# A four-layer diffusion trunk in fp32: norming shared by two engines, epilogue banks released sooner, adaLN chunks placed anew

## The chip, the cores and the metric

The kernel runs on one core of a Trainium2 chip. The metric is the device time of one execution in microseconds (us); the figure for the kernel before is the median of three runs. The engines are TensorE (PE), VectorE (DVE), ScalarE (ACT), GpSimd (POOL) and SyncE (SP), which here only issues loads and stores.

## What is computed

One inference step of a trunk with 128 context tokens and 256 latent tokens (384 columns), D = 1024, four layers. The token mixers are a chunked gMLP (layers 0 and 3), a pooling mixer (layer 1) and a windowed attention (layer 2); each is followed by a gated ConvFFN. Cut to what matters here:

```python
def ada_params(cond, w, b):
    m = jax.nn.silu(cond) @ w + b
    return jnp.split(m[:, None, :], 6, axis=-1)

def conv_ffn(h, w_in, conv_w, conv_b, w_out):
    a, u = jnp.split(h @ w_in, 2, axis=-1)
    ap = jnp.pad(a, ((0, 0), (1, 1), (0, 0)))
    a = ap[:, :-2] * conv_w[0] + ap[:, 1:-1] * conv_w[1] + ap[:, 2:] * conv_w[2] + conv_b
    return (jax.nn.gelu(a) * u) @ w_out
...
        sh1, sc1, gt1, sh2, sc2, gt2 = ada_params(cond, w_ada[i], b_ada[i])
        h = rms_norm(x, g_mix[i]) * (1 + sc1) + sh1
...
        x = x + gt1 * y
        h = rms_norm(x, g_ffn[i]) * (1 + sc2) + sh2
        x = x + gt2 * conv_ffn(h, w_ffn_in[i], ffn_conv_w[i], ffn_conv_b[i], w_ffn_out[i])
```

Context and latent tokens have their own `cond`, so every adaLN vector has two columns.

## The kernel before, in words

Activations lie transposed: x is eight blocks k of 128 features by 384 tokens. All weights are cut by the host into 582 chunks of 128x1024 fp32 (512 KB) in one list, `chunk_plan`, and SP loads them in that order into five raw buffers (`load`, a buffer is free again when its reader is done). To keep fp32 accuracy, a chunk is split: ScalarE copies it to fp32r (`whi`, line 347), VectorE subtracts (`wlo`, line 354), four buffers each; activations are split the same way, and `mm3` (line 669) makes three products, whi x hi, wlo x hi, whi x lo. `w_get` hands out a split chunk and keeps the splits three chunks ahead.

adaLN weights are chunks of the same list that need no split. An "ad" chunk is read by VectorE, two multiplications with a sum per chunk (`ada_dve`, line 389). An "ap" chunk is multiplied on TensorE, four products of 32 columns (`ada_pe`, line 407), its row being turned at the end; its raw buffer is held until TensorE's program comes to it. The table `ADA` says which chunks (kind, layer, which of the six vectors, which of eight blocks) go into which phase; `weave` spreads them between the phase's weight chunks, and `EDGES` says how many weight chunks at its begin and end stay free of them. Phases are named (layer, name): gv, gu and go are the gMLP's, fi is the ffn's first product, fo its second.

The ffn (`ffn`) makes 22 blocks f of a and u, 128 features each; a pair of PSUM banks (pa, pu) holds one f, and there are six such banks. A step of an f is 48 products. To start before the norm of x is known, f = 0, 1 (four "fr" chunks, two blocks k in each) and f = 2 run on raw h, which is x times the gain, with two more columns in which the shift is carried; rows of these three are scaled by rbs, the reciprocal root mean square, in the epilogue. At k = stat_k the sum of squares is taken over the partitions by products with ones (`stats`, line 530: last square and accumulator apart, six matmuls, two passes each) and turned into a diagonal R; at stat_k + 2 `spread` (line 545) gives rbs to all partitions. From then on `norm` writes normed h, block by block (`put_act`: VectorE x times rbs, line 578; ScalarE gain and shift, line 580, and the fp32r part, line 581; VectorE the rest, line 582), for f = 3 to 21. Blocks are done in pairs: two puts, then two rests.

The epilogue of an f stands in the instruction order of the next f: `epi_a` (f < 3: lines 695 and 699 scale a and u out of the banks, line 697 copies the two shift columns of a), `epi_b` (the convolution, lines 710 to 716, named ct), `epi_c` (gelu; gg, line 726, reads u in its bank; for f < 3 line 730 reads the two shift columns of u in its bank), then gg is split. Since f = 0 and 1 come out together, the epilogues run two f behind until f = 8, where one step holds two of them. So f+3 takes the banks of f.

At the start SP loads x, three weights and the parameters; cond goes through Silu, squares of x are summed, and the first block's shift and gain come from `a0` products on TensorE.

Of the kernel before, what the change touches and what calls it, by code (L numbers as in the profile page):

```python
# [1655 lines left out]
```

## Time and profile before

| | us |
|---|---|
| median of 3 runs | 1843.94 (1841.29 to 1845.10) |
| the profiled execution, its own time | 1845.28 |
| its span, first to last instruction | 1843.5 |
| TensorE busy in it | 1762.9 (96%) |
| VectorE busy | 1383.0 (75%) |
| ScalarE busy | 884.9 (48%) |
| mean granted clock of TensorE | 0.983 of 2.4 GHz |

The profile is one execution. Busy time is the share in which an engine has an instruction under way; a wait is idle time, put down to the instruction that ended it. Times inside the profile count from the span's start. fp32 products appear as two passes each, products of fp32r as one.

### The profile page before, as it was taken

To read this page: it belongs to the slowest core of one execution; us is meant where nothing else is said; L and a number is where in the kernel's file an instruction comes from. 1 tells how busy PE (TensorE), PEld (TensorE's weight loads), DVE (VectorE), ACT (ScalarE), POOL (GpSimd) and SP (SyncE) were. 2 spreads that over 40 slices of the span, in tenths; PEclk is the share of its full clock that TensorE was granted. 3 is DMA by queue.
4 is the path that set the end of the run, shared out by engine and by line. 5 is a ranking of instruction groups with operands and counts; after the bars stand their busy time and mean duration, and the time that the engine had idled before them with its cause. 6 is when DMAs were issued, how large, how long until landed. Compare 5 with 4: busy or idle time off the path is not lost.

```text
span 1843.5 us, 26653 instructions
## 1 busy us (share of the span) xinstructions
PE 1762.9 (96%) x10128; PEld 1683.5 (91%) x10128; DVE 1383.0 (75%) x2364; ACT 884.9 (48%) x1637; POOL 1.8 (0%) x30
## 2 busy tenths in 40 slices
PE   7999989999999699999998989999999999899999
PEld 5799989999998699899777979999988999899999
DVE  5887969888985688888688678877776776676632
ACT  3644354444444644542468564543354444654531
POOL 0000000000000000000000000000000000000000
PEclk9999999999999899999999999999999999899999
DMA  8864635565662255566550335555546344244441
GB/s 323 279 210 150 206 113 184 187 202 189 234 218 97 92 194 196 192 202 226 198 177 13 126 106 192 193 167 200 183 147 208 115 138 149 103 154 162 136 137 63
DMA packets 87635, 311.62 MB, mean 169 GB/s; under 512 B 10450, under 2 KB 10962, under 8 KB 87252
## 3 DMA queue, kind: packets, MB, share of 16 engines
q1 hardware_dynamic: 87364, 309.92, 49.7%
q8 instruction: 79, 1.29, 0.3%
q14 instruction: 48, 0.39, 0.1%
q10 hardware_dynamic: 144, 0.01, 0.0%
HBM read 308.06 MB, written 1.84 MB: 168 GB/s over the span
## 4 chain that ended last, share of the span: by engine, by line
PE 68%; DVE 19%; ACT 9%; issue 3%; DMA 1%; DVEq 0%; ACTq 0%
PE mm L669 51%; DVE junk L389 6%; PE mm L834 6%; DVE wlo L354 5%; DVE ct L716 3%; ACT whi L347 2%; ACT nt L580 2%; PE S L669 1%; PE mm L878 1%; ACT hb L581 1%; ACT gg L725 1%; DVE gl L587 1%; PE adaT L669 1%; PE S L1109 1%; DMA wraw<-wts 1%
## 5 line engine op out<-in xcount | busy, mean ns | idle before, releaser
L669 PE MATMUL mm<-hb,whi 128*128 128x384 f32 (+1 forms) x4064 | 902.3, 341 | 49.7 <-DVE gg L730 27.0
L669 PEld LDWEIGHTS mm<-hb,whi 128*128 128x128 f32 x4064 | 731.9, 191 | 57.2 <-issue 28.4
L354 DVE TENSOR_TENSOR wlo<-wraw,whi 128x1024 fp32r<-128x1024 f32 (+2 forms) x390 | 466.7, 1201 | 223.8 <-ACT whi L347 222.7
L347 ACT ACTIVATE whi<-wraw 128x1024 fp32r<-128x1024 f32 (+2 forms) x390 | 400.1, 1034 | 276.4 <-PE mm L669 185.2
L669 PE MATMUL mm<-hb,wlo 128*128 128x384 f32 (+1 forms) x2032 | 527.1, 340 | 4.4 <-DVE wlo L354 4.3
L389 DVE SCALAR_TENSOR_TENSOR junk<-wraw,condb 128x1024 bf16<-128x1024 f32 x320 | 391.0, 1222 | 8.4 <-ACT condb L1574 2.7
L669 PEld LDWEIGHTS mm<-hb,wlo 128*128 128x128 f32 x2032 | 373.4, 191 | 6.9 <-DVE wlo L354 6.9
L725 ACT ACTIVATE gg<-ct 128x128 f32<-128x128 f32 (+1 forms) x152 | 47.0, 356 | 273.4 <-DVE ct L716 273.4
L669 PE MATMUL mm<-gh,whi 128*128 128x384 f32 x448 | 124.1, 338 | 2.5 <-ACT whi L347 2.5
L669 PE MATMUL mm<-gh,wlo 128*128 128x384 f32 x448 | 124.0, 338 | 0.8 <-DVE wlo L354 0.8
L669 PE MATMUL mm<-gl,whi 128*128 128x384 f32 x448 | 123.8, 337 | 0.0
L716 DVE SCALAR_TENSOR_TENSOR ct<-ab,par,ct 128x385 f32<-128x385 f32 x176 | 108.8, 620 | 7.9 <-ACT ct L714 4.2
L605 ACT ACTIVATE hb<-x,A 128x128 fp32r<-128x128 f32 x96 | 43.2, 457 | 102.9 <-DVE x L462 92.0
L834 PE MATMUL mm<-whi,hb 128*128 128x512 f32 x320 | 87.5, 399 | 0.0
L669 PEld LDWEIGHTS mm<-gh,whi 128*128 128x128 f32 x448 | 82.2, 189 | 2.9 <-ACT whi L347 2.9
L669 PEld LDWEIGHTS mm<-gh,wlo 128*128 128x128 f32 x448 | 82.4, 189 | 1.1 <-DVE wlo L354 1.1
L669 PEld LDWEIGHTS mm<-gl,whi 128*128 128x128 f32 x448 | 82.3, 189 | 0.0
L726 DVE TENSOR_TENSOR gg<-mm,gg 128x384 f32<-128x384 f32 x76 | 42.4, 558 | 47.4 <-ACT gg L725 46.7
L834 PEld LDWEIGHTS mm<-whi,hb 128*128 128x128 f32 x320 | 60.6, 190 | 15.9 <-ACT rb L1560 0.8
L714 ACT ACTIVATE ct<-ab,par 128x385 f32<-128x385 f32 x88 | 62.7, 712 | 3.4
L462 DVE SCALAR_TENSOR_TENSOR x<-mm,prm,x 128x128 f32<-128x128 f32 x92 | 33.6, 411 | 27.4 <-PE mm L669 27.3
L607 DVE SCALAR_TENSOR_TENSOR hb<-x,A,hb 128x128 fp32r<-128x128 f32 x96 | 40.2, 418 | 9.9 <-ACT hb L605 0.9
(276 smaller groups left out, 1648.5 us busy)
## 6 DMA issues: line engine op xcount, KB each, us to landing
wraw<-wts SPq DMA_DIRECT2D x562, 512.0 KB, 3.9
wraw<-wts SPq DMA_DIRECT2D x12, 256.0 KB, 3.1
wraw<-wts SPq DMA_DIRECT2D x8, 384.0 KB, 4.2
x<-x SPq DMA_DIRECT2D x4, 384.0 KB, 4.5
mx<-mix SPq DMA_DIRECT2D x1, 1280.0 KB, 8.1
y<-x SPq DMA_DIRECT2D x3, 384.0 KB, 4.2
condb<-condb SPq DMA_DIRECT2D x1, 1024.0 KB, 8.3
ws<-a_w_s SPq DMA_DIRECT2D x2, 512.0 KB, 4.0
```

The source lines that it names most:

```text
L347: nc.scalar.activation(hi[:, :n], t[:, :n], AF.Copy)
L354: nc.vector.tensor_tensor(out=lo[:, :n], in0=t[:, :n], in1=hi[:, :n].bitcast(F32), op=ALU.subtract)
L389: nc.vector.scalar_tensor_tensor(out=self.junk.bitcast(BF16), in0=w, scalar=1.0, in1=self.condb[:, c, :], op0=ALU.mult, op1=ALU.mult, accu ...
L580: nc.scalar.activation(t[:, t0:t1], t[:, t0:t1], AF.Identity, scale=A[:, k, c:c + 1], bias=sh[:, k, c:c + 1])
L605: nc.scalar.activation(self.hh[:, d, t0:t1], self.x[:, d, t0:t1], AF.Copy, scale=A[:, d, c:c + 1])
L607: nc.vector.scalar_tensor_tensor(out=self.hl[:, d, t0:t1], in0=self.x[:, d, t0:t1], scalar=A[:, d, c:c + 1], in1=self.hh[:, d, t0:t1].bitc ...
L669: nc.tensor.matmul(o, w[:, c:c + nw], r, start=(first and p == 0), stop=(last and p == 2))
L714: nc.scalar.activation(t, ab[:, 1:T + 2], AF.Identity, scale=cw[1], bias=cb)
L716: nc.vector.scalar_tensor_tensor(out=t, in0=ab[:, i:i + T + 1], scalar=cw[i], in1=t, op0=ALU.mult, op1=ALU.add)
L725: nc.scalar.activation(g[:, t0:t1], t[:, t0 + c:t1 + c], GELU)
L726: nc.vector.tensor_tensor(out=g, in0=u, in1=g, op=ALU.mult)
L834: nc.tensor.matmul(ps[n][i], hs, w[p == 1][:, c:c + 512], start=(k == 0 and p == 0), stop=(k == 7 and p == 2))
```

## The change

1. `norming` writes normed h. Even blocks k are made as before; for odd ones VectorE multiplies by gain and rbs (two pieces, since context and latent differ), ScalarE adds the shift into the fp32r part, and VectorE makes the rest in two pieces. The rest of block k-1 is issued behind the put of block k.
2. `stat_k` goes from 3 to 2, and in layer 1 from 6 to 4.
3. The last square is added to acc on VectorE (`add_square`), so `stats` takes three matmuls for six, in the four ffns and layer 3's gMLP.
4. be is four wide: ScalarE copies the shift columns of u as well, and line 730's successor reads them from there.
5. The step with two epilogues is f = 5 and no longer f = 8.
6. `ADA` and `EDGES`: (0,go) 9 to 12 ad and 8 ap, (0,fi) 26 to 18, (0,fo) 19 to 16, (1,fi) 24 to 18, (1,fo) 16 to 22 ad; 582 chunks as before.
7. At the start: ones first, Silu's table loaded by a dummy, the small constant sel loaded from ScalarE's queue, and 25, 3 and 5 fp32 products of ones into a spare bank ahead of the first a0 products, the stats and the first turned row.

```diff
 ADA = {
@@
-    (0, "go"): [("ad", 0, 3, 2, 8), ("ad", 0, 5, 0, 3)],
-    (0, "fi"): [("ad", 0, 5, 3, 8), ("ad", 1, 1), ("ad", 1, 2), ("ad", 1, 0, 0, 5)],
-    (0, "fo"): [("ad", 1, 0, 5, 8), ("ad", 1, 4), ("ad", 1, 3)],
-    (1, "fi"): [("ad", 1, 5), ("ad", 2, 1), ("ad", 2, 0)],
-    (1, "fo"): [("ad", 2, 4), ("ad", 2, 3)],
+    (0, "go"): [("ad", 0, 3, 2, 8), ("ad", 0, 5, 0, 6), ("ap", 1, 1)],
+    (0, "fi"): [("ad", 0, 5, 6, 8), ("ad", 1, 2), ("ad", 1, 0)],
+    (0, "fo"): [("ad", 1, 4), ("ad", 1, 3)],
+    (1, "fi"): [("ad", 1, 5), ("ad", 2, 1), ("ad", 2, 0, 0, 2)],
+    (1, "fo"): [("ad", 2, 0, 2, 8), ("ad", 2, 4), ("ad", 2, 3)],
@@
-EDGES = {(0, "gv"): (2, 1), (0, "go"): (5, 0), (3, "gv"): (5, 2), "fi": (8, 4), (3, "go"): (5, 2)}
+EDGES = {(0, "gv"): (2, 1), (0, "go"): (5, 0), (3, "gv"): (5, 2), "fi": (8, 2), (3, "go"): (5, 2)}
+WARM = (25, 3, 5)
@@
+    def add_square(self, pr):
+        self.nc.vector.tensor_tensor(out=pr["acc"], in0=pr["acc"], in1=pr["sq"], op=ALU.add)
@@
-    def put_act(self, k, A, rbs, hi, lo, sh):
+    def put_one(self, k, A, rbs, hi, lo, sh, act):
         nc = self.nc
         t = self.tmp.tile([128, T], F32, tag="sq", name="nt")
...
         for c, (t0, t1) in enumerate(GRPS):
+            nc.vector.scalar_tensor_tensor(out=t[:, t0:t1], in0=self.x[:, k, t0:t1], scalar=A[:, k, c:c + 1],
+                                           in1=rbs[:, t0:t1], op0=ALU.mult, op1=ALU.mult)
+            nc.scalar.activation(hi[:, k, t0:t1], t[:, t0:t1], AF.Identity, bias=sh[:, k, c:c + 1])
+        def last():
+            for c, (t0, t1) in enumerate(GRPS):
+                nc.vector.scalar_tensor_tensor(out=lo[:, k, t0:t1], in0=t[:, t0:t1], scalar=sh[:, k, c:c + 1],
+                                               in1=hi[:, k, t0:t1].bitcast(F32), op0=ALU.add, op1=ALU.subtract)
+        return last
@@
-                be = self.tmp.tile([128, 2], F32, tag="be", name="be")
-                nc.scalar.activation(be, pa[:, T:TE], AF.Copy)
+                be = self.tmp.tile([128, 4], F32, tag="be", name="be")
+                nc.scalar.activation(be[:, 0:2], pa[:, T:TE], AF.Copy)
+                nc.scalar.activation(be[:, 2:4], pu[:, T:TE], AF.Copy)
@@
-                return f, a1, be, u1, pu[:, T:TE]
+                return f, a1, be, u1, be[:, 2:4]
@@
-            def norm(n):
-                ks, to_norm[:] = to_norm[:n], to_norm[n:]
-                for i in range(0, len(ks), 2):
-                    for lo in [self.put_act(k, pr["A"], rbs, nh, nl, sh) for k in ks[i:i + 2]]:
-                        lo()
+            def norming():
+                last = None
+                for k in range(KD):
+                    this = self.put_one(k, pr["A"], rbs, nh, nl, sh, k % 2 == 0)
+                    if last is not None:
+                        last()
+                    last = this
+                    yield
+                last()
+            steps = norming()
+            def norm(n):
+                for _ in range(n):
+                    next(steps, None)
+            self.add_square(pr)
@@
-                        R = self.diag(self.stats(pr["acc"], pr["sq"]))
+                        R = self.diag(self.stats(pr["acc"]))
@@
-                now, prev = (prev, []) if f == 8 else (prev[:1], prev[1:])
+                now, prev = (prev, []) if f == 5 else (prev[:1], prev[1:])
@@
         nc.scalar.dma_start(cin, a["cond"])
+        nc.scalar.dma_start(self.cst[:, 512:514], a["cst"][:, 512:514])
...
-        nc.sync.dma_start(self.cst[:, 512:514], a["cst"][:, 512:514])
         self.load()
+        nc.vector.memset(self.ones, 1.0)
...
+        nc.scalar.activation(self.tmp.tile([128, 1], F32, tag="dmy", name="dmy", bufs=1), self.ones[:, 0:1], AF.Silu)
+        spare = self.bank("spare")
+        def warm(n):
+            for _ in range(WARM[n]):
+                nc.tensor.matmul(spare[:, 0:128], self.ones, self.ones, start=True, stop=True)
+        warm(0)
...
+        def first_stats():
+            warm(1)
+            r.append(self.stats(acc))
+        a0_mm(0, first_stats)
+        warm(2)
@@
-            pr = self.ffn(l, pr, follow, 6 if kind == 1 else 3)
+            pr = self.ffn(l, pr, follow, 4 if kind == 1 else 2)
```

The order of VectorE at the norming of layer 2's ffn, before (nt and hb are the put and the rest, a and u the first epilogue):

```order
L578 TENSOR_TENSOR nt<-x,rbs 128x384 x2
L582 TENSOR_TENSOR hb_84<-nt,hb_84 128x384 x2
L354 TENSOR_TENSOR wlo<-wraw,whi 128x1024
L578 TENSOR_TENSOR nt<-x,rbs 128x384 x2
L582 TENSOR_TENSOR hb_84<-nt,hb_84 128x384 x2
L578 TENSOR_TENSOR nt<-x,rbs 128x384 x2
L582 TENSOR_TENSOR hb_84<-nt,hb_84 128x384 x2
L578 TENSOR_TENSOR nt<-x,rbs 128x384 x2
L582 TENSOR_TENSOR hb_84<-nt,hb_84 128x384 x2
L695 TENSOR_TENSOR a_2457<-mm,rbs 128x384
L699 TENSOR_TENSOR u_2461<-mm,rbs 128x384
L354 TENSOR_TENSOR wlo<-wraw,whi 128x1024
```

And after the change, the same place:

```order
L585 TENSOR_TENSOR nt<-x,rbs 128x384
L598 SCALAR_TENSOR_TENSOR hb_84<-nt,prm,hb_84 128x128
L598 SCALAR_TENSOR_TENSOR hb_84<-nt,prm,hb_84 128x256
L592 SCALAR_TENSOR_TENSOR nt<-x,A,rbs 128x128
L592 SCALAR_TENSOR_TENSOR nt<-x,A,rbs 128x256
L589 TENSOR_TENSOR hb_84<-nt,hb_84 128x384
L585 TENSOR_TENSOR nt<-x,rbs 128x384
L598 SCALAR_TENSOR_TENSOR hb_84<-nt,prm,hb_84 128x128
L598 SCALAR_TENSOR_TENSOR hb_84<-nt,prm,hb_84 128x256
L592 SCALAR_TENSOR_TENSOR nt<-x,A,rbs 128x128
L592 SCALAR_TENSOR_TENSOR nt<-x,A,rbs 128x256
L589 TENSOR_TENSOR hb_84<-nt,hb_84 128x384
```

The puts of two blocks stood together, then their rests; now each rest stands behind the next block's put, and every second block has two instructions for one.

The order of VectorE from the third epilogue's end into the step that holds two, layer 2, after the change (line 736 is ct, 746 gg, 391 an adaLN chunk, 606 the rest of gg):

```order
L356 TENSOR_TENSOR wlo<-wraw,whi 128x1024
L606 TENSOR_TENSOR gl<-gg,gh 128x384
L356 TENSOR_TENSOR wlo<-wraw,whi 128x1024
L391 SCALAR_TENSOR_TENSOR junk,prm<-wraw,condb 128x1024 x2
L736 SCALAR_TENSOR_TENSOR ct<-ab_2354,par,ct 128x385 x2
L736 SCALAR_TENSOR_TENSOR ct<-ab_2353,par,ct 128x385 x2
L746 TENSOR_TENSOR gg<-mm,gg 128x384 x2
L356 TENSOR_TENSOR wlo<-wraw,whi 128x1024
L606 TENSOR_TENSOR gl<-gg,gh 128x384 x2
L356 TENSOR_TENSOR wlo<-wraw,whi 128x1024
```

Before, f=5's step held one ct and one gg, and the like rows with two of them stood at f=8:

```order
L354 TENSOR_TENSOR wlo<-wraw,whi 128x1024
L389 SCALAR_TENSOR_TENSOR junk,prm<-wraw,condb 128x1024 x2
L716 SCALAR_TENSOR_TENSOR ct<-ab_2250,par,ct 128x385 x2
L716 SCALAR_TENSOR_TENSOR ct<-ab_2251,par,ct 128x385 x2
L726 TENSOR_TENSOR gg<-mm,gg 128x384 x2
L354 TENSOR_TENSOR wlo<-wraw,whi 128x1024
L389 SCALAR_TENSOR_TENSOR junk,prm<-wraw,condb 128x1024 x2
L587 TENSOR_TENSOR gl<-gg,gh 128x384 x2
```

The two epilogues at once now belong to f = 3 and 4 and no longer to f = 6 and 7.

The order of TensorE at the kernel's begin, after the change (spare is the bank of the products of ones, psa the a0 products, cs the stats, a0T the turned row):

```order
L1534 MATMUL spare<-ones 128x128 x25
L1550 MATMUL psa<-wraw,cond 32x256 x4
L1534 MATMUL spare<-ones 128x128 x3
L536 MATMUL cs<-ones,acc 128x1 x3
L1550 MATMUL psa<-wraw,cond 32x256 x4
L1534 MATMUL spare<-ones 128x128 x5
L1564 MATMUL a0T<-cst,a0row 128x2 x2
L551 MATMUL mm<-R,ones 128x384
L1550 MATMUL psa<-wraw,cond 32x256 x8
```

Line 1534's rows are new there; the others kept their order.

## Rows read from the trace of the kernel before

**Rows 1.** The page: busy times, VectorE's group of line 389, the weights' DMA issues.

```profile
PE 1762.9 (96%) x10128; PEld 1683.5 (91%) x10128; DVE 1383.0 (75%) x2364; ACT 884.9 (48%) x1637; POOL 1.8 (0%) x30
...
L389 DVE SCALAR_TENSOR_TENSOR junk<-wraw,condb 128x1024 bf16<-128x1024 f32 x320 | 391.0, 1222 | 8.4 <-ACT condb L1574 2.7
...
wraw<-wts SPq DMA_DIRECT2D x562, 512.0 KB, 3.9
```

**Rows 2.** TensorE's waits: line, releaser, total us, times, longest.

```profile
PE mm L669 <- DVE gg L730: 27.0, 7, 8.7
PE mm L669 <- ACT be L697: 13.1, 3, 4.4
...
PE mm L669 <- ACT whi L347: 7.2, 6, 2.5
PE mm L669 <- DVE wlo L354: 5.1, 8, 0.8
PE mm L669 <- DVE gg L726: 4.8, 3, 1.9
```

**Rows 3.** TensorE's timeline, layer 1's f=4, layer 2's f=3: start, us, [idle before].

```profile
632.45 0.66 PE L669 MATMUL mm<-hb,whi 128*128 128x384 f32 x1 [5.33 <-DVE gg L730]
...
1080.92 0.45 PE L669 MATMUL mm<-hb,whi 128*128 128x384 f32 x1 [4.38 <-ACT be L697]
```

**Rows 4.** VectorE's timeline, norming in layer 2.

```profile
1062.19 1.03 DVE L578 TENSOR_TENSOR nt<-x,rbs 128x384 f32<-128x384 f32 x2 [0.93 <-ACT rbs L752]
...
1067.89 1.02 DVE L578 TENSOR_TENSOR nt<-x,rbs 128x384 f32<-128x384 f32 x2
...
1071.97 1.02 DVE L578 TENSOR_TENSOR nt<-x,rbs 128x384 f32<-128x384 f32 x2
```

**Rows 5.** ScalarE's timeline, the same place.

```profile
1062.79 0.99 ACT L580 ACTIVATE nt<-nt,prm,A 128x128 f32<-128x128 f32 x2 [0.63 <-DVE nt L578]
1063.81 0.52 ACT L581 ACTIVATE hb<-nt 128x384 fp32r<-128x384 f32 x1
```

**Rows 6.** Busy times by stretch: us, each engine (instructions), clock, DMA share, GB/s.

```profile
272.70:453.90 181.20, 167.56 (x913) 163.70 (x914) 158.83 (x242) 84.99 (x165) 0.00 (x0) 0.95 0.57 192
453.90:551.00 97.10, 93.74 (x531) 93.16 (x531) 86.90 (x145) 40.95 (x68) 0.00 (x0) 0.98 0.64 215
620.00:640.00 20.00, 14.66 (x69) 14.38 (x69) 15.94 (x27) 10.59 (x20) 0.00 (x0) 0.81 0.36 123
795.40:887.00 91.60, 91.60 (x532) 91.31 (x534) 71.93 (x112) 28.38 (x38) 0.00 (x0) 1.00 0.64 211
```

**Rows 7.** VectorE's timeline, the first block of layer 0's gMLP.

```profile
16.31 0.74 DVE L565 SCALAR_TENSOR_TENSOR nt<-x,A,mm 128x128 f32<-128x128 f32 x2 [0.72 <-PE mm L545]
17.13 0.98 DVE L570 SCALAR_TENSOR_TENSOR hb<-nt,prm,hb 128x128 fp32r<-128x128 f32 x2
```

**Rows 8.** VectorE's timeline, the ffn's epilogues in layer 2.

```profile
1080.11 0.55 DVE L695 TENSOR_TENSOR a<-mm,rbs 128x384 f32<-128x384 f32 x1
...
1104.93 1.22 DVE L354 TENSOR_TENSOR wlo<-wraw,whi 128x1024 fp32r<-128x1024 f32 x1
...
1129.52 1.23 DVE L354 TENSOR_TENSOR wlo<-wraw,whi 128x1024 fp32r<-128x1024 f32 x1 [0.16 <-ACT whi L347]
...
1135.45 0.55 DVE L726 TENSOR_TENSOR gg<-mm,gg 128x384 f32<-128x384 f32 x1
```

**Rows 9.** TensorE's timeline, adaLN chunks at layer 2's begin.

```profile
886.80 1.50 PE L407 MATMUL psa<-wraw,cond 128*32 128x256 f32 x24
```

**Rows 10.** Busy times of line 530 in layer 2's ffn; the counts are passes.

```profile
1055.23:1056.50 1.27, 1.27 (x12) 1.27 (x12) 1.00 0.60 200
```

**Rows 11.** ScalarE's timeline, start.

```profile
4.71 1.28 ACT L1540 ACT_TABLE_LOAD   x1 [4.71 <-DMA cin<-cond]
```

**Rows 12.** TensorE's timeline, start.

```profile
8.77 1.08 PE L1512 MATMUL psa<-wraw,cond 128*32 128x256 f32 x8 [8.77 <-DMA wraw<-wts]
...
18.07 2.26 PE L834 MATMUL mm<-whi,hb 128*128 128x512 f32 x5
```

More of the change, by code (lines that the diff above doesn't have):

```diff
@@ L572, in put @@
                                                op0=ALU.add, op1=ALU.subtract)
-    def put_act(self, k, A, rbs, hi, lo, sh):
+    def put_one(self, k, A, rbs, hi, lo, sh, act):
         nc = self.nc
         t = self.tmp.tile([128, T], F32, tag="sq", name="nt")
-        nc.vector.tensor_tensor(out=t, in0=self.x[:, k, :], in1=rbs, op=ALU.mult)
-        for c, (t0, t1) in enumerate(GRPS):
-            nc.scalar.activation(t[:, t0:t1], t[:, t0:t1], AF.Identity, scale=A[:, k, c:c + 1], bias=sh[:, k, c:c + 1])
-        nc.scalar.activation(hi[:, k, :], t, AF.Copy)
-        return lambda: nc.vector.tensor_tensor(out=lo[:, k, :], in0=t, in1=hi[:, k, :].bitcast(F32), op=ALU.subtract)
+        if act:
+            nc.vector.tensor_tensor(out=t, in0=self.x[:, k, :], in1=rbs, op=ALU.mult)
+            for c, (t0, t1) in enumerate(GRPS):
+                nc.scalar.activation(t[:, t0:t1], t[:, t0:t1], AF.Identity, scale=A[:, k, c:c + 1], bias=sh[:, k, c:c + 1])
+            nc.scalar.activation(hi[:, k, :], t, AF.Copy)
+            return lambda: nc.vector.tensor_tensor(out=lo[:, k, :], in0=t, in1=hi[:, k, :].bitcast(F32),
+                                                   op=ALU.subtract)
+        for c, (t0, t1) in enumerate(GRPS):
+            nc.vector.scalar_tensor_tensor(out=t[:, t0:t1], in0=self.x[:, k, t0:t1], scalar=A[:, k, c:c + 1],
+                                           in1=rbs[:, t0:t1], op0=ALU.mult, op1=ALU.mult)
+            nc.scalar.activation(hi[:, k, t0:t1], t[:, t0:t1], AF.Identity, bias=sh[:, k, c:c + 1])
+        def last():
+            for c, (t0, t1) in enumerate(GRPS):
+                nc.vector.scalar_tensor_tensor(out=lo[:, k, t0:t1], in0=t[:, t0:t1], scalar=sh[:, k, c:c + 1],
+                                               in1=hi[:, k, t0:t1].bitcast(F32), op0=ALU.add, op1=ALU.subtract)
+        return last
     def split_act(self, src, hi, lo):
@@ L757, in ffn @@
                         norm(2)
-            if R is not None:
-                nc.scalar.activation(rbs, self.spread(R), AF.Copy)
-            norm(2)
             prev = [(0, b[0], b[1]), (1, b[2], b[3])]
@@ L783, in ffn @@
                 prev.append((f, pa, pu))
-            assert not to_norm and len(prev) == 1
+            assert next(steps, 0) == 0 and len(prev) == 1
             sts = []
@@ L905, in gmlp @@
             else:
+                self.add_square(pr)
                 b = [self.bank()[:, :TE] for _ in range(4)]
@@ L916, in gmlp @@
                         if k == 2:
-                            R = self.diag(self.stats(pr["acc"], pr["sq"]))
+                            R = self.diag(self.stats(pr["acc"]))
                         if k == 4:
@@ L1493, in run @@
         nc.sync.dma_start(self.par, a["par"])
-        nc.sync.dma_start(self.cst[:, 512:514], a["cst"][:, 512:514])
         self.load()
+        nc.vector.memset(self.ones, 1.0)
         nc.vector.memset(self.cond, 0.0)
-        nc.vector.memset(self.ones, 1.0)
         make_identity(nc, self.ident)
+        nc.scalar.activation(self.tmp.tile([128, 1], F32, tag="dmy", name="dmy", bufs=1), self.ones[:, 0:1], AF.Silu)
[4 more added lines that the diff above has]
+        warm(0)
         sel = self.cst[:, 512:514]
@@ L1552, in run @@
         r = []
-        a0_mm(0, lambda: r.append(self.stats(acc)))
+        def first_stats():
[3 more added lines that the diff above has]
+        warm(2)
         R = []
```

5 lines of the change are left out of this document (2 added, 3 removed).

## The prediction, made before the changed kernel ran

> **What bounds the kernel now.** I began with the page's busy times: TensorE is at work for 96% of the span, VectorE for 75%, ScalarE for 48% [rows 1]. So time can only leave where TensorE waits, where its clock is low, or where it does work that can go. The waits of PE come next [rows 2]: 27.0 us until VectorE's gg of line 730, 13.1 until ScalarE's be of line 697, 4.8 until gg of line 726, 7.2 and 5.1 until a weight's split. The first three, 44.9 us, are one place in four layers: the ffn's first steps on normed h. The timelines show it [rows 3]: in layer 2, f=3 waits 4.38 us for a bank that epi_a of f=0 had to read, and a like wait follows for the bank that line 730 still reads as a scalar; in layer 1, f=4 waits 5.33. What is late is VectorE's own queue: the norming of eight blocks stands ahead of f=0's epilogue, its pairs 4.08 us apart [rows 4]. In such a pair VectorE works 1.02+2×0.56 and a further idle part goes to ScalarE's chain, 0.99 and 0.52 a block [rows 5]: the two engines wait for each other in turn.
>
> Then the clock: in 620 to 640 the granted mean is 0.81 [rows 6], a stretch at 1.2 instead of 2.4 GHz after the wait of 5.33 [rows 3]. Of 20×0.19=3.8 us, 1.2 fell into the wait itself, so 2.6 were lost. Six such stretches stand around the 44.9 us, 13.9 us together, read the same way.
>
> The last 12.3 (7.2+5.1) lie in the ffns of layers 0 and 1, where VectorE is busy 158.83 of 181.20 us and 86.90 of 97.10 [rows 6]; layer 1's fo, with 71.93 of 91.60, has none. A line-389 chunk is two passes of 1.222 [rows 1] and a reading of the sum, 2.46 us of VectorE.
>
> **The change, part by part.** TensorE's step of an f: layer 1's fo is 8×22×3=528 products in 91.60 us [rows 6], 0.1735 each; 48 of them are 8.33, three steps 25.0. A raw block k is 12 products of 386 columns, 2.1.
>
> (1) *Norming and statistics, layer 2.* Statistics one block sooner and shorter take 2.1+0.65 off; VectorE's queue hands about 1.1 of it back (a whole split now stands behind R), so the first put is at about 1060.55 instead of 1062.19 [rows 4]. An odd block costs VectorE 0.74+0.98 [rows 7] and ScalarE two pieces, like the 0.99 [rows 5]; an even one VectorE 0.47 (half of two starts in 1.02) and 0.56, ScalarE 0.99+0.52. A pair is 2.75 on VectorE and 2.5 on ScalarE; pipelined one block behind, VectorE's sum decides. Four pairs 11.0, the split in between 1.14, about 1 for the first block's chain: 13.1 instead of 17.9. So f=0's epilogue starts at 1073.65 instead of 1080.11 [rows 8], and with be four wide both banks are free after its two reads. TensorE, which ended f=2 at 1080.92-4.38=1076.5, now does at 1075.9, 2.2 after that start: both waits of f=3 go.
>
> The Trainium skill's page "VectorE: DVE Perf Modes" (Rules for kernel authors) says to keep the number of vector instructions down; by it the odd blocks, four instructions for two, are a loss. The rows above bear out the price, 1.72 against 1.03 a block, and the sum holds it.
>
> (2) *What is late next.* The catch-up step, two epilogues in one, moves from f=8 to f=5, and f=6 needs the banks of f=3, which that step frees. Before, three steps took VectorE from 1080.11 to 1104.93, 24.82, and the double step from its start to its first gg's end 1135.45+0.55-1129.52=6.48 [rows 8]: 31.3. TensorE leaves 25.0 plus the 2.2. So f=6 waits 4.1 in layer 2. In layer 0 there is a chunk more (32.4: it waits 5.2), in layer 3 one fewer (28.3: 1.1). Layer 1 gets its rbs late still: four puts before f=2's epilogue, four behind; by the same steps f=3 to f=5 wait 4.0 and f=6 6.1. Clock after them, at 2.6 (1.7, as the shorter stretches, where less): 2.6, 4.3, 2.6, 1.7. Sum, layer by layer, 7.8+14.4+6.7+2.8=31.7 where 44.9+13.9=58.8 stood: **-27.1**. Ends: no wait at f=6, -53; the norming no faster, about -2.
>
> (3) *Fewer chunks per phase.* (0,fi) 26 to 18, (0,fo) 19 to 16, (1,fi) 24 to 18. VectorE per f falls in layer 0 from 9.1 (1.6 chunks) to 8.1, under 8.33, so the small waits go: the 12.3 and three stretches of low clock behind them, 1.7, 3.4 and 1.7: **-19.1**. End: half of it stays, since 8.1 of 8.33 leaves no room.
>
> (4) *Where the chunks went.* (1,fo) gets 22: 71.93+7×2.46=89.2 of 91.60 (15 fell into that stretch before). The nearest row is (0,fo) at 86.90, which lost 3.4 in waits and 1.7 in clock, though it was entered with a backlog. I take **+4**, ends 0 and 9. (0,go) takes three more ad, 68 of about 74 us: **+1**. Eight chunks go to TensorE there: 24 products in 1.50 [rows 9] are three chunks, 0.50 each, 4.0, with the turned row at the end **+4.6**.
>
> (5) *Squares joined.* A 0.56 add on VectorE, beside TensorE's products of the chunk before, and six passes instead of twelve: twelve keep TensorE 1.27 [rows 10], 0.65 saved, five times: **-3.3**.
>
> (6) *Start.* The Silu table's 1.28 [rows 11] leave the head of ScalarE's queue, so squares wait for x alone: acc about 0.8 sooner. Eight products of the first weight took 1.08 there [rows 12] where twenty-four like ones take 1.50 later [rows 9]: half speed. If the products of ones raise the clock, the stats, spread and a0 products up to 18.07 [rows 12] give 1.7 more: **-2.5**. Ends: -3, and +0.5 if the speed stays: 25 products of two passes, at half speed some 0.21 apiece (twice the 1.27/12 of [rows 10]), then last to 11 or 12, past 8.77. The small load sel goes from SP's queue to ScalarE's, ahead of Silu, and the third weight's load, behind it on SP, now waits for cond's: both lie beside the loads of x and of two weights that TensorE waits for anyway; without that cover they would use up the 0.8.
>
> On the table load the Trainium skill's page "ScalarE: Activation LUTs" (What ACT_TABLE_LOAD costs) adds a drain and comes to 2.66 us a switch; by it this term would be an estimated 1.4 larger. The load's row shows 1.28 and no drain, and the sum goes by it.
>
> The be copy on ScalarE (two columns, 12 times more) costs nothing: ScalarE is at 48% and the banks' other readers end later; without that cover, 0.2 a time in three steps of a layer.
>
> Sum: -27.1-19.1+4+1+4.6-3.3-2.5=-42.4. The profiled execution was 1845.28: 1802.9. It lies 1.3 over the median of 1843.94, so 1801.6, **1802 us**; own range 1791 to 1814.
>
> **The rivals.**
> A. *The f=5 catch-up is no stall.* If VectorE's first three steps are shorter than I read (in layer 2 some of 24.82 was ScalarE's chain and the chunk sits a step later), f=6 finds its banks free. For: idle parts in VectorE's steps. Against: the step has four ct in it. Gain 5.2+6.1+4.1+1.1 and 9.5 of clock, 26: 1776.
> B. *VectorE becomes the bound where the chunks now lie.* Half of the 19.1 stays and (1,fo) pays 9 instead of 4: 1802+9.5+5=1816.5. For: 89.2 of 91.6. Against: layer 2's lighter phases without waits.
> C. *The norming stays as slow*, since two nt buffers make each put wait for the lo before it. Then epi_a comes 1.64 sooner only; f=3 waits some 3, f=6 some 6: 4.9 more a layer and 1.4 of clock, 25: 1827. The Trainium skill's rule on instruction counts, above, would have it so.
> D. *Starved ring in (0,go), slower.* A chunk for TensorE keeps one of five raw buffers until TensorE comes to it, and the splits then run two chunks ahead instead of three. From issue to landing are 3.9 [rows 1], a split's VectorE half is 1.23 [rows 8] and ScalarE's, ahead of it, about as long, and a chunk on VectorE in front 2.46: 8.8 of some 12 us at two chunks ahead. If that does not suffice, each of eight chunks holds TensorE up. From 5.3 us a time, clock included, the 42.4 are gone; at 5 and 1.7 it is 1802+54=1856. Against: 3 us of slack.
>
> That the change does not do what it says: only the products of ones could fail so, which is (6)'s end.
>
> **How the numbers follow.** Forecast 0.47, A 0.16, B 0.20, C 0.10, D 0.07. The range 1773 to 1827 holds nearly all of the forecast and B, a good half of A and near half of C, 0.8 in all. What a measurement of this kernel can tell from no change is about 0.2%, 3.7 us. Slower by more: most of D, 0.04. Within: D's shallow end and C's tail, 0.03. Faster 0.93.
>
> **What would show it.** Right: no wait of f=3 for be or for line 730's successor; line 714's first a about 13 us after the first nt; a wait of 4 to 6 us at f=6 in layers 0 to 2, about 1 in layer 3, ended by gg of line 746; no split waits in (0,fi) and (1,fi); spread's matmul in the start near 0.85. Wrong: first a 16 us or more after the nt (C); f=6 without a wait (A); splits waited for in (1,fo) (B) or in (0,go) (D).

## The result

The changed kernel takes 1787.91 us, median of 4 runs (1786.50 to 1789.28), where the kernel before took 1844.52 beside it; the ratio is 0.9695 with a 95% interval of 0.9678 to 0.9712. That is 56.6 us less, inside the range of 1773 to 1827, and 14 below the forecast of 1802. The profiled execution has a span of 1786.6 us where 1843.5 stood; TensorE is busy 98% of it (96% before), VectorE 77%, ScalarE 49%, mean clock 0.996 (0.983).

In one of the experiments (e9_k2) two of four executions, the profiled one among them, ran disturbed, 37 us longer in stretches that the edit does not touch; its ratio is from the other two.

### The profile after

TensorE's waits (line, releaser, total us, times, longest), answering to [rows 2]; of the 44.9 us until an epilogue nothing stands at the head any more:

```profile
PE mm L688 <- ACT whi L349: 5.7, 4, 2.6
PE mm L688 <- DVE wlo L356: 3.2, 5, 0.8
PE psa L1550 <- DMA wraw<-wts: 2.7, 3, 1.7
PE mm L688 <- DVE hb L589: 2.3, 1, 2.3
PE cs L536 <- DVE acc L484: 2.1, 1, 2.1
...
PE mm L688 <- ACT ab L732: 1.0, 2, 0.6
```

The waits for splits (5.7 and 3.2) are still there, but elsewhere, as the timelines put it: 2.6 and 0.8 at the end of layer 0's go, the rest in layer 1's fo. The 2.1 until acc are layer 0's stats. A wait for gg (line 746, or line 750 for f < 3) is in no row, not even at f=6. The last row is f=6's: in layers 0 and 1 its second product waits 0.49 and 0.55 us, until ScalarE's ab (line 732) has read a bank:

```profile
309.25 0.44 PE L688 MATMUL mm<-hb,whi 128*128 128x384 f32 x1 [0.49 <-ACT ab L732]
```

Busy times by stretch (us, TensorE, its weight loads, VectorE, ScalarE, POOL, with the instructions in brackets, then clock, DMA share, GB/s), answering to [rows 6]: layer 0's go, fi and fo, and layer 1's fo.

```profile
171.40:254.30 82.90, 79.50 (x475) 73.48 (x474) 65.25 (x112) 27.11 (x43) 0.27 (x6) 0.96 0.63 213
283.50:442.40 158.90, 158.41 (x914) 158.09 (x913) 138.12 (x206) 82.64 (x162) 0.00 (x0) 1.00 0.56 188
442.40:534.40 92.00, 91.69 (x529) 91.37 (x528) 81.56 (x136) 42.49 (x71) 0.00 (x0) 1.00 0.63 212
753.80:853.80 100.00, 94.74 (x529) 92.68 (x527) 87.88 (x140) 29.61 (x41) 0.00 (x0) 0.98 0.69 234
```

fi takes 158.9 us where it took 181.2 and more, with VectorE at 138.12 of them. Layer 1's fo takes 100.00 with VectorE at 87.88, where it took 91.60 at 71.93. go takes 82.90; it took 69.7 in the trace of before, from 171.0 to 240.7.

VectorE's timeline in layer 2's ffn (start, us), answering to [rows 4] and [rows 8]: the first put, the first epilogue, the step with two, and two single steps after it.

```profile
1027.59 0.55 DVE L585 TENSOR_TENSOR nt<-x,rbs 128x384 f32<-128x384 f32 x1
1028.06 0.75 DVE L592 SCALAR_TENSOR_TENSOR nt<-x,A,rbs 128x128 f32<-128x128 f32 x2
...
1030.36 0.56 DVE L585 TENSOR_TENSOR nt<-x,rbs 128x384 f32<-128x384 f32 x1
1030.83 0.74 DVE L598 SCALAR_TENSOR_TENSOR hb<-nt,prm,hb 128x128 fp32r<-128x128 f32 x2
...
1041.09 0.56 DVE L714 TENSOR_TENSOR a<-mm,rbs 128x384 f32<-128x384 f32 x1
...
1066.95 1.22 DVE L356 TENSOR_TENSOR wlo<-wraw,whi 128x1024 fp32r<-128x1024 f32 x1
1068.09 2.46 DVE L736 SCALAR_TENSOR_TENSOR ct<-ab,par,ct 128x385 f32<-128x385 f32 x4
1070.46 0.55 DVE L746 TENSOR_TENSOR gg<-mm,gg 128x384 f32<-128x384 f32 x1
...
1072.19 1.23 DVE L356 TENSOR_TENSOR wlo<-wraw,whi 128x1024 fp32r<-128x1024 f32 x1 [0.40 <-ACT whi L349]
...
1079.77 0.56 DVE L746 TENSOR_TENSOR gg<-mm,gg 128x384 f32<-128x384 f32 x1 [0.68 <-ACT gg L745]
...
1087.84 0.56 DVE L746 TENSOR_TENSOR gg<-mm,gg 128x384 f32<-128x384 f32 x1 [0.68 <-ACT gg L745]
```

The first a stands 13.50 us behind the first nt (forecast 13.1, before 17.92), and the first gg of the double step ends at 1071.0, 29.9 behind the first a (forecast 31.3). A single step with one adaLN chunk in it, gg to gg, is 8.07 us, and in each VectorE stands idle some 1.1 of them for ScalarE (0.40 and 0.68 in these rows).

ScalarE's and TensorE's timelines at the same place:

```profile
1064.16 0.53 ACT L732 ACTIVATE ab<-mm 128x128 f32<-128x128 f32 x2
...
1065.34 0.53 ACT L732 ACTIVATE ab<-mm 128x128 f32<-128x128 f32 x2
```

```profile
1042.39 0.87 PE L688 MATMUL mm<-hb,whi 128*128 128x386 f32 x4
...
1067.36 0.86 PE L688 MATMUL mm<-hb,whi 128*128 128x384 f32 x4
1068.06 0.51 PE L688 MATMUL mm<-hb,wlo 128*128 128x384 f32 x2
```

f=3 starts at 1042.74, with the third product of the first row, without a wait, and f=6, three steps of 8.32 later, at 1067.71, with the third of the row of 1067.36, 2.8 us before gg of f=3 has even begun. What it did need was ready: line 732's ab of f=3 and f=4 ended at 1064.7 and 1065.9.

### The account by stretch

Each column is one execution. Boundaries are the first and the last product on raw h (386 columns) and the 912th after it; fr is f = 0 to 2, fi f = 3 to 21 with the waits in front. The two columns in the middle are experiments, told below: the new tables alone (e11_tableonly), and all but the tables (e3_oldada).

| stretch, us | before | tables alone | all but tables | changed |
|---|---|---|---|---|
| start, layer 0's gMLP | 240.7 | 253.2 | 239.2 | 254.3 |
| layer 0 fr | 27.5 | 27.5 | 26.8 | 29.1 |
| layer 0 fi | 185.5 | 168.7 | 181.2 | 158.9 |
| layer 0 fo, pool | 126.4 | 120.9 | 124.8 | 121.5 |
| layer 1 fr | 27.6 | 27.6 | 26.9 | 26.9 |
| layer 1 fi | 187.5 | 176.8 | 179.2 | 163.0 |
| layer 1 fo, attention | 253.7 | 257.2 | 253.7 | 262.2 |
| layer 2 fr | 27.5 | 27.5 | 26.8 | 26.8 |
| layer 2 fi | 168.3 | 168.5 | 158.6 | 158.1 |
| layer 2 fo | 91.5 | 91.5 | 91.5 | 91.5 |
| layer 3 gMLP | 214.7 | 214.8 | 214.1 | 214.1 |
| layer 3 fr | 27.5 | 27.5 | 26.8 | 26.8 |
| layer 3 fi | 169.7 | 169.8 | 158.1 | 158.1 |
| layer 3 fo, end | 95.3 | 95.3 | 95.3 | 95.3 |
| span | 1843.5 | 1826.7 | 1803.1 | 1786.6 |

158.1 is a fi without any loss: 19 steps of 8.32. One execution differs from the next in layer 0: up to its f=3 the changed kernel and three experiments whose edits lie behind that point (e1_pairs, e2_f8, e8_l1) took 283.5, 281.4, 285.7 and 281.3 us.

### The profile page after: what moved, and what is told of

Its sections match the earlier page's. It is cut to its first block, busy times and chain, and to the rows that moved or that the text cites. A ratio compares the mean times of both kernels' runs of the same rounds, so it can differ in the third digit from the quotient of the medians.

```text
span 1786.6 us, 26835 instructions
## 1 busy us (share of the span) xinstructions
PE 1754.6 (98%) x10230; PEld 1675.2 (94%) x10230; DVE 1371.8 (77%) x2369; ACT 872.2 (49%) x1635; POOL 1.8 (0%) x30
## 4 chain that ended last, share of the span: by engine, by line
PE 61%; DVE 22%; ACT 8%; issue 5%; DMA 4%; SPq 0%; DVEq 0%; ACTq 0%
PE mm L688 45%; DVE wlo L356 7%; DVE junk L391 7%; PE mm L862 6%; DMA wraw<-wts 4%; ACT whi L349 3%; DVE ct L736 3%; PE S L688 1%; PE mm L906 1%; ACT gg L745 1%; DVE gl L606 1%; PE adaT L688 1%; PE S L1138 1%; PE adaT L862 1%; PE psa L862 1%
## 5 line engine op out<-in xcount | busy, mean ns | idle before, releaser
L688 PE MATMUL mm<-hb,whi 128*128 128x384 f32 (+1 forms) x4064 | 888.7, 338 | 6.6 <-ACT whi L349 2.6
L688 PEld LDWEIGHTS mm<-hb,whi 128*128 128x128 f32 x4064 | 722.7, 189 | 11.6 <-ACT whi L349 3.3
L688 PE MATMUL mm<-hb,wlo 128*128 128x384 f32 (+1 forms) x2032 | 521.4, 337 | 0.8 <-DVE wlo L356 0.8
L391 DVE SCALAR_TENSOR_TENSOR junk<-wraw,condb 128x1024 bf16<-128x1024 f32 x304 | 371.6, 1222 | 9.1 <-ACT condb L1618 2.7
L688 PEld LDWEIGHTS mm<-hb,wlo 128*128 128x128 f32 x2032 | 369.1, 189 | 1.3 <-DVE wlo L356 1.3
L746 DVE TENSOR_TENSOR gg<-mm,gg 128x384 f32<-128x384 f32 x76 | 42.4, 558 | 47.4 <-ACT gg L745 46.7
L862 PE MATMUL mm<-wlo,hb 128*128 128x512 f32 x160 | 47.8, 405 | 0.0
```

Of the source, the lines that this page charges most:

```text
L391: nc.vector.scalar_tensor_tensor(out=self.junk.bitcast(BF16), in0=w, scalar=1.0, in1=self.condb[:, c, :], op0=ALU.mult, op1=ALU.mult, accu ...
L688: nc.tensor.matmul(o, w[:, c:c + nw], r, start=(first and p == 0), stop=(last and p == 2))
L746: nc.vector.tensor_tensor(out=g, in0=u, in1=g, op=ALU.mult)
L862: nc.tensor.matmul(ps[n][i], hs, w[p == 1][:, c:c + 512], start=(k == 0 and p == 0), stop=(k == 7 and p == 2))
```

## The experiments

Each is the changed kernel with one edit, unless said otherwise. Medians stand beside 1787.91, and what an edit gives back is its worth beside all the other parts, so the worths don't add up to the 56.6; where a few us decide, the ratios to the kernel before, taken on the same chip, stand beside 0.9695.

**Why f=6 did not wait (e1_pairs).** The pool of banks gives out the one that was released first. Behind single steps that is a pair of one f; the double step releases both a banks (after ScalarE's ab), then both u banks (after gg). So f=6 gets the a banks of f=3 and f=4. The edit takes six banks once and keeps the pairs together:

```diff
-            b = [self.bank()[:, :TE] for _ in range(4)]
+            six = [self.bank() for _ in range(6)]
+            b = [t[:, :TE] for t in six[:4]]
...
-                pa, pu = self.bank()[:, :w0], self.bank()[:, :w0]
+                pa, pu = (six[2 * (f % 3) + i][:, :w0] for i in range(2))
```

> The ffn takes its six banks once and gives f the pair f mod 3 (in the changed kernel the pool hands out the bank that was released first, so behind the double step f=6 gets the a banks of f=3 and f=4, which only ScalarE's ab reads). Theory, the order of release hides f=6's wait: f=6 now waits for gg of f=3, by the changed kernel's trace 5.7, 5.8, 3.1 and 0.7 us in layers 0 to 3, with the clock behind them some 7 us more; the whole goes from 1787.9 to about 1809. Rival, VectorE was simply early enough at f=6: no wait, 1788.

1804.16 us (ratio 0.9775, 0.9759 to 0.9792). TensorE's waits, and its timeline at f=6 of layer 0:

```profile
PE mm L688 <- DVE gg L746: 15.0, 4, 5.8
```

```profile
312.33 0.69 PE L688 MATMUL mm<-hb,whi 128*128 128x384 f32 x1 [5.63 <-DVE gg L746]
312.82 0.84 PE L688 MATMUL mm<-hb,wlo 128*128 128x384 f32 x2
313.46 1.49 PE L688 MATMUL mm<-hb,whi 128*128 128x384 f32 x4
...
317.21 0.86 PE L688 MATMUL mm<-hb,whi 128*128 128x384 f32 x4
```

The four waits are 5.63, 5.76, 3.02 and 0.60 us, each within 0.1 of what was worked out. The two products of 312.82 take 0.64 to the next start, later pairs 0.35: half speed up to about 317. The four fi together take 21.1 us more (7.3, 7.0, 5.9 and 0.9), 15.0 of it waits and about 6 low clock behind them, near the 7 expected. The whole loses only 16 (15.1 in the traces), because 6 us come back elsewhere: layer 1's fo and attention take 3.4 less, with one pair of waits for splits in fo where the changed kernel has three, and layer 0 up to f=3 and its fo take 2.7 less, no more than executions differ there. Why layer 1's fo gains was not tried. The prediction's times for VectorE were right within 1.1 us a layer; its bank was wrong.

**The place of the double step (e2_f8).**

```diff
-                now, prev = (prev, []) if f == 5 else (prev[:1], prev[1:])
+                now, prev = (prev, []) if f == 8 else (prev[:1], prev[1:])
```

> The double step goes back to f=8, the rest as changed. Theory (order of release): single steps free both banks of f=3 last with gg, so f=6 waits for it, some 4.5, 4.6, 2 and 0 us in layers 0 to 3, and about 6 us of clock: about 1804. Rival, the place of the double step does not matter because VectorE catches up either way: 1788.

1804.41 (0.9774, 0.9756 to 0.9792). Four waits until gg of line 746 at f=6, 5.16, 5.28, 2.58 and 0.2:

```profile
PE mm L688 <- DVE gg L746: 13.2, 4, 5.3
```

The rival's 1788 falls. That f=5 is worth 16 us here rests on the same release order: with the double step at f=8, f=6 gets banks that gg of f=3 reads last. Other steps than these two were not tried.

**The norming (e4_oldnorm)**, puts and rests in pairs as before:

```diff
-                last = None
-                for k in range(KD):
-                    this = self.put_one(k, pr["A"], rbs, nh, nl, sh, k % 2 == 0)
-                    if last is not None:
-                        last()
-                    last = this
-                    yield
-                last()
+                for k in range(0, KD, 2):
+                    rests = [self.put_one(i, pr["A"], rbs, nh, nl, sh, True) for i in (k, k + 1)]
+                    for r in rests:
+                        r()
+                    yield
+                    yield
```

> Norming in pairs with all puts as in the kernel before (each block one multiplication on VectorE, three activations), the rest as changed. Theory, the norming sets when f=0's epilogue starts: first a 17.9 instead of 13.5 us after the first nt, f=3 waits about 2.7 us in layers 0, 2 and 3 and more in layer 1, and a stretch of low clock in some: 1800 to 1810. Rival, the copy of the shift columns and the double step did it all: 1788.

1808.96 (0.9801, 0.9784 to 0.9819). VectorE's puts and first a in layer 2, and TensorE's waits:

```profile
1036.05 1.02 DVE L585 TENSOR_TENSOR nt<-x,rbs 128x384 f32<-128x384 f32 x2
...
1040.12 1.02 DVE L585 TENSOR_TENSOR nt<-x,rbs 128x384 f32<-128x384 f32 x2
...
1053.95 0.55 DVE L714 TENSOR_TENSOR a<-mm,rbs 128x384 f32<-128x384 f32 x1
```

```profile
PE mm L688 <- ACT be L717: 14.0, 4, 3.9
```

The first a is 17.90 behind the first nt again, and f=3 waits 3.35, 3.40 and 3.40 in layers 0, 2 and 3 and f=4 3.86 in layer 1. So the norming is worth 21 us in this company, and rival C is out by the 13.50. The edit takes back two things at once, the order one block behind and the second form of the odd blocks; what each of them is worth was not tried.

**The copy of the shift columns (e6_be2)**, be two wide and line 750 reading u's columns in the bank (`return f, a1, be, u1, pu[:, T:TE]`; the copy in layer 3's gMLP goes back as well).

> be two wide again, so line 750 reads u's shift columns in the bank. Theory: the second product of f=3 waits for gg of f=0, in layer 2 until 1046.5 where TensorE is ready at 1042.9, 3.6 us, likewise in layers 0 and 3, with 2 to 3 us of clock each; in layer 1 gg of f=1 comes behind the last puts, at f=4: about 1812 (1806 to 1818). Rival, the norming alone pulled the epilogue far enough: below 1792.

1803.96 (0.9774, 0.9758 to 0.9790), a little under the expected range (line 749 is the changed kernel's 750):

```profile
PE mm L688 <- DVE gg L749: 16.9, 5, 6.1
```

3.51 in layers 0, 2 and 3, 6.08 in layer 1, as expected. The four fi lose 20.7 us by it, more than the waits, so low clock was paid too; the total is 16 because layer 1's fo and attention take 5.4 less, again with one pair of split waits for three. One activation of two columns more in three steps of a layer buys 16 us.

**The tables (e3_oldada)**: `ADA` and `EDGES` of the kernel before, the rest as changed.

> The tables of the kernel before for the adaLN chunks, the rest as changed. Theory from the account by phase: the ffns of layers 0 and 1 and layer 0's fo lose the 19 us of small waits and clock again, and layer 0's go and layer 1's fo get back 13 to 15 and 8.5: nearly level, 1784 to 1791. Rival, the table carries the gain in the ffns (VectorE's lighter load is what takes f=3 to f=6 off the path): 1807 or more.

1808.29 (0.9797, 0.9781 to 0.9813): the rival's number, and my account was wrong. The rival's reason holds in small part only: for an epilogue's bank TensorE waits 4.0 us in two places; the rest is mostly waits for splits. Busy times of fi in layers 0 and 1, and TensorE's waits:

```profile
266.00:447.20 181.20, 165.41 (x913) 158.75 (x913) 159.18 (x242) 84.15 (x166) 0.00 (x0) 0.99 0.60 192
599.00:778.10 179.10, 165.73 (x914) 160.26 (x913) 155.14 (x239) 85.63 (x169) 0.00 (x0) 0.98 0.58 183
```

```profile
PE mm L688 <- ACT whi L349: 14.5, 15, 2.5
PE mm L688 <- DVE wlo L356: 10.4, 16, 0.8
```

With the epilogue's stalls gone fi of layer 0 takes 181.20 us still: the whole kernel has 24.9 us of waits for splits, where 12.3 stood before [rows 2]. VectorE is busy only 159.18 of the 181.20 and is the bound all the same. fi has 44 weight chunks, two to a step; the old `EDGES` leave 32 of them, 16 steps, for 26 adaLN chunks, 1.6 a step. From the 8.07 of a step with one, that is 8.07+0.6×2.46=9.5, and 16 of these with three of 8.3 are 178. The new table lays 18 into 17 steps, 8.2 a step, under TensorE's 8.32. So the limit is about one chunk a step and not a share of busy time. The reading is that the microsecond that VectorE spends waiting for ScalarE in every step cannot hold a chunk; no run took that idle time away. Before, the stalls at f=3 to f=8 had given VectorE part of what it lacked: layer 0's first split wait came at 396.04, and here it comes at 311.46. So the 12.3 read there were too small for what the tables are worth.

**The tables alone (e11_tableonly)**, the kernel before with the new `ADA` and `EDGES`.

> The kernel before with the new tables alone (chunks placed as in the changed kernel, norming, stats, be, double step and start as before). If the two parts add up, it is before less the 19 that the tables are worth in the changed kernel (1808 against 1788): 1826. Rival, they overlap: with the old epilogue the waits at f=3 let VectorE catch up, so the small waits that the tables remove are mostly given already, while go and layer 1's fo pay in full: 1838 to 1846.

1828.63 (ratio 0.9915, 0.9900 to 0.9929), 15.7 us less than before. The two parts nearly add up: 16.8 and 40.4 us of span in the traces, together 57.2, measured 56.9; by the medians 15.7 and 37.0, together 52.7, measured 56.6, where each has an interval of some 3 either way. By stretch they do not: in the fi of layers 0 and 1 the parts alone bring 21.1 and 19.0 and together 26.6 and 24.5, and layer 1's fo costs 3.5 alone and 8.5 together. The rival's 1838 to 1846 is out.

**Layer 0's go (e7_goearly)**, `(0, "go"): (2, 2)` for `(5, 0)` in `EDGES`.

> Layer 0's go: its adaLN chunks spread with two weight chunks free at its begin and two at its end, for five and none. Theory: the 13 us that go lost and the 2 of the stats behind it come half from TensorE's own eight chunks (6 us) and half from VectorE's crowd of chunks at the end (waits of 2.6, 0.8 and 2.1 and 3.2 of clock); spreading takes the second half away: 1779 to 1782. Rival, VectorE's total load in go is the bound: 1787 or more.

1784.14 (0.9670, 0.9656 to 0.9685): 4 us, half of what I expected, and between the expected range and the rival's. Up to f=3 layer 0 takes 278.8 instead of 283.5 (281.3 to 285.7 in the four traces above); the stats' wait is gone, the split waits at go's end are smaller, but go itself still takes far more than before.

**Layer 1's fo (e8_l1)**: four chunks back to fi, 18 to 22 there and 22 to 18 in fo.

```diff
-    (1, "fi"): [("ad", 1, 5), ("ad", 2, 1), ("ad", 2, 0, 0, 2)],
-    (1, "fo"): [("ad", 2, 0, 2, 8), ("ad", 2, 4), ("ad", 2, 3)],
+    (1, "fi"): [("ad", 1, 5), ("ad", 2, 1), ("ad", 2, 0, 0, 6)],
+    (1, "fo"): [("ad", 2, 0, 6, 8), ("ad", 2, 4), ("ad", 2, 3)],
```

> Four chunks of layer 2's vector 0 go back from layer 1's fo (22 to 18) to its fi (18 to 22). Theory: fo loses its three pairs of split waits and most of its 8.5 us, fi with VectorE near 149 of 163 us stays as it is: 1780 to 1783. Rival, fi's VectorE has no room and pays the same there: 1787 or more.

1788.04 (0.9691, 0.9677 to 0.9705), no difference, and the rival's number: fo and the attention give 6.0, fi takes 8.4, 171.4 where 163.0 stood; 2.6 less in layer 0's stretches, which the edit does not touch, make it even. So beyond one chunk a step a chunk costs fi 2.1 us, near its 2.46 of VectorE, though VectorE shows 147.38 of 171:

```profile
590.00:761.00 171.00, 161.78 (x911) 157.10 (x911) 147.38 (x226) 84.18 (x165) 0.00 (x0) 1.00 0.57 183
```

**Layer 1's statistics (e9_k2)**, the go edges above and `self.ffn(l, pr, follow, 2)` in all layers.

> The go edges of the run before (2 and 2) and stat_k = 2 in layer 1 too. Theory: layer 1's sum of squares is done at 567.9 in the changed kernel's trace, where TensorE reaches k=2 at 568.1, so nothing waits for it, all puts stand ahead of f=3, and layer 1's fi falls from 163.0 to the 158.1 of layers 2 and 3: 4.8 less than the run with the go edges, 1779. Rival, VectorE is still behind there (residual, split) and the stats wait or f=3 does: 1783 or more.

Ratio 0.9647 (0.9625 to 0.9670), 1779 us against 1844.28 beside it, from two executions (1777.54 and 1781.43), as expected; fi of layer 1 takes 158.7, in e10_at's trace too. The forecast of layer 1's remaining loss was too dark, and what was left of it was stat_k.

**Chunks on TensorE elsewhere (e10_at, e12_apfo).** e10_at builds on e9_k2:

```diff
-    (1, "fo"): [("ad", 2, 0, 2, 8), ("ad", 2, 4), ("ad", 2, 3)],
+    (1, "fo"): [("ad", 2, 0, 2, 8), ("ad", 2, 4)],
-    (2, "at"): [("ap", 2, 5)],
+    (2, "at"): [("ap", 2, 3), ("ap", 2, 5)],
-FILL = (2, 2, 1, 1, 1, 1, 1)
+FILL = (3, 3, 2, 2, 2, 2, 2)
```

> As the run with stat_k = 2, and layer 2's vector 3 as eight TensorE chunks in its attention in place of eight VectorE chunks in layer 1's fo (22 to 14), with more chunks taken per head there. Theory: fo gets back its 8.5 us, the attention pays 0.5 a chunk, some in TensorE's waits of about 8 us there: 3.5 to 6 less, 1773 to 1776. Rival, the eight chunks hold raw buffers and delay the o weights or the heads: 1779 or more.

1774.78 (0.9618, 0.9602 to 0.9634), within the expected range and 13 us faster than the changed kernel (`FILL` is the number of chunks taken per head). e12_apfo builds on e10_at: go has no TensorE chunks, `("ap", 1, 0)` stands in layer 0's fo (twelve weight chunks from its end kept free), `("ad", 1, 1), ("ad", 1, 2)` in its fi.

> As the run with eight chunks in the attention, and layer 1's eight TensorE chunks moved from layer 0's go to its fo (vector 0 instead of 1, since fo may still use it late; vector 1 goes to VectorE in fi). Theory, in go the eight chunks cost more than TensorE's 0.5 to 0.8 each because they hold raw buffers next to twelve VectorE chunks in only sixteen weight chunks, where fo has sixteen in twenty-four: up to f=3 layer 0 takes 266 to 270 instead of 278.4, fo 6 more: 1768 to 1772. Rival, a TensorE chunk costs the same anywhere: 1774 to 1776, or above if fo's VectorE fills up.

1774.23 (0.9615, 0.9602 to 0.9628), the same as e10_at, so above the expected range and on the rival's number. Busy times of go, first in e12_apfo, then in e10_at:

```profile
171.40:240.00 68.60, 68.26 (x394) 67.83 (x394) 64.13 (x111) 26.82 (x43) 0.27 (x6) 1.00 0.62 202
```

```profile
171.40:251.40 80.00, 76.84 (x462) 70.89 (x462) 64.95 (x114) 27.89 (x44) 0.27 (x6) 0.98 0.70 227
```

Without the eight chunks go takes 68.60 us with twelve VectorE chunks in it, so those are free, and up to f=3 layer 0 takes 266.9 instead of 278.4, as the theory had it. fo pays 9.7 and not 6, though: 2.3 of split waits, with clock 4, and 0.7 a chunk. So a TensorE chunk costs 0.7 and what it does to the splits around it: 1.4 in go and 1.2 in fo, nearly the same in both, as the rival had it, and more than twice the forecast's price. What it does shows in go's waits of SP's load (line 330) and of ScalarE's split, in the changed kernel (171.4 to 254.3) and, the last row, in e12_apfo (171.4 to 240.0):

```profile
SPq L330 <- PE psa L409: 15.0, 6, 4.1
...
ACT whi L349 <- DMA wraw<-wts: 22.4, 6, 5.7
```

```profile
ACT whi L349 <- DMA wraw<-wts: 5.1, 1, 5.1
```

The loads wait 15.0 us for buffers that TensorE's chunks still hold, a row that e12_apfo's go has not, and the splits then wait for the loads. A ring of another size was not tried. Over fo and the pooling mixer behind it the splits wait for loads as long with the eight chunks as without them (27.2 and 27.8 us), so what they cost there beyond 0.7 is not explained.

**The start (e5_oldstart)**: products of ones, dummy activation and sel's place undone, cond zeroed before ones.

> The start as before: no products of ones, no early Silu table, sel on SP's queue, cond zeroed before ones. Theory, what the start gains up to the first product of gr (15.68 against 18.07 us) is given back at the wait for the second half of the third a0 weight and the low clock behind it, since the weights' loads set the pace: 1788, within 1 us. Rival, the start is worth its 2.5 us: 1790.5.

1789.51 (0.9700, 0.9685 to 0.9714): the intervals overlap, so 1.6 us is told neither from nothing nor from the rival's 2.5, and up to f=3 the two spans are 283.8 and 283.5. The changed kernel's timeline shows where the gain goes:

```profile
1.04 7.43 PE L1534 MATMUL spare<-ones 128*128 128x128 f32 x50 [1.04 <-DVE ones L1525]
9.08 0.64 PE L1550 MATMUL psa<-wraw,cond 128*32 128x256 f32 x8 [0.61 <-DMA wraw<-wts]
...
15.68 1.67 PE L862 MATMUL mm<-whi,hb 128*128 128x512 f32 x6
...
20.15 0.64 PE L1550 MATMUL psa<-wraw,cond 128*32 128x256 f32 x8 [1.73 <-DMA wraw<-wts]
20.72 2.33 PE L862 MATMUL mm<-wlo,hb 128*128 128x512 f32 x6
...
28.00 1.66 PE L862 MATMUL mm<-wlo,hb 128*128 128x512 f32 x6
```

The first a0 products take 0.64 and not 1.08 [rows 12], and the first product of gr comes at 15.68 and not at 18.07; but the third a0 weight lands when it lands, TensorE waits 1.73 for it, and the six products behind it take 2.33 where the next six of the kind take 1.66. The first product behind the last a0 row starts at 55.66 in the changed kernel, at 55.29 in the kernel before and at 54.45 in e5_oldstart. The changed kernel's trace is a late case: in the eleven traces with the new start it comes at 53.6 to 56.1, in the middle at 53.9, and in the three with the old one at 54.5 to 55.3. So the start gains about 1 us there at most times, of the 2.4 at the first product of gr.

## Why the prediction was right, and where it was off

The direction and the place held, and so did the mechanism of (1): the ffn's first steps were VectorE's queue, and what takes f=0's epilogue forward frees TensorE (e4_oldnorm, e6_be2). The terms were off by more than the sum shows. Of the signs named for being wrong three came: f=6 without a wait for gg, split waits in layer 1's fo, and split waits in layer 0's go.

By its own steps, from the table above: the four rows of fi and layer 0's fo lose 77.8 us together. How much of it is (1), (2) and how much (3) depends on which comes first, and the middle columns give both orders: the tables alone 32.7 in these five rows and the rest behind them 45.1, or all but the tables 35.5 and the tables behind it 42.3. (4) is 8.5 in layer 1's fo, and in layer 0 up to f=3 the 13.6 and 1.6 of the first two rows, with (5)'s 0.7 added and (6)'s 0.4 taken off: 15.5. (6) is 55.66 against 55.29, one trace each.

| step | forecast | measured |
|---|---|---|
| (1), (2) f=3 to f=6, clock with it | -27.1 | -35.5 to -45.1 |
| (3) fewer chunks in fi and layer 0's fo | -19.1 | -42.3 to -32.7 |
| (1) to (3) together | -46.2 | -77.8 |
| (4) go, its stats, layer 1's fo | +9.6 | +24.0 |
| (5) squares joined | -3.3 | -3.4 |
| (6) start | -2.5 | +0.4 |
| sum | -42.4 | -56.8 |

So (1) to (3) brought 31.6 us more than forecast and (4) cost 14.4 more, and the two errors partly cancel. That is luck: with (4) as forecast the kernel would have taken about 1773.5, the lower end of the range.

(1) 13.50 for 13.1 us of norming, both waits of f=3 gone in layers 0, 2 and 3. With e4_oldnorm the 17.9 are back. The Trainium skill's page "VectorE: DVE Perf Modes" (Rules for kernel authors) wants the count of instructions kept down; in this trace VectorE has more of them and is done 4.4 us sooner, since its idle time between the first put and the first a fell from 8.5 to 2.7 us. What stat_k = 2 gives by itself in layers 0, 2 and 3 was not tried.

(2) The step that failed is "f=6 needs the banks of f=3, which that step frees". f=6 needs the first two banks that are released, and those are a banks, which ScalarE's ab leaves long before gg; its only waits there are the 0.49 and 0.55 us for ab. Rival A had the outcome and not the reason: VectorE was nearly as late as forecast, e1_pairs gives 15.0 us of waits where 16.5 were worked out, and 21.1 us in the four fi. Layer 1 kept 4.9 of its loss, 2.26 of it for the last block's normed h, not 14.4.

(3) Undersized: the 12.3 of waits read before were what the epilogue's stalls had left. e3_oldada shows 24.9 once those are gone.

(4) Undersized as well. Layer 1's fo paid 8.5, near the upper end of 9 that stood there. In go twelve VectorE chunks are free (e12_apfo), the forecast's +1 was no more than that, and the eight TensorE chunks cost 15.5 with the stats' wait behind them (11.5 where the others are spread better) and not 4.6: the row [rows 9] prices three chunks in a row, 0.50 each, with nothing to be split around them. Rival D's mechanism, buffers held until TensorE comes to them, is in the trace (15.0 us of the loads' waits), at about a quarter of the price that D put on it; B happened in layer 1's fo and not in the fi.

(5) Right: 0.7 an ffn. In layer 0 the stats then waited 2.1 for VectorE's crowd in go, which e7_goearly removes.

(6) The first product of gr comes 2.4 sooner as forecast, and the wait for the third weight takes back about half of it within 5 us, in this trace with the low clock behind it all; of the whole kernel's time e5_oldstart can't tell it from nothing. On the estimate by the Trainium skill's page "ScalarE: Activation LUTs" (1.4 more): this trace shows no drain at the table load either; it takes 1.28 at 1.63, and the next activation starts at 2.93.
